# Bias, compression and state space parameters laid out by the host as their tiles lie

## The chip, the cores and the metric

The kernel runs on one core of a Trainium2 chip. The metric is the device time of one execution in microseconds (us), as the median of several runs. A core has five engines that run beside one another: TensorE (PE, matrix products; its weight loads are shown apart as PEld), VectorE (DVE), ScalarE (ACT), GpSimd (POOL) and SyncE (SP), which here issues all transfers between the DRAM and the core's memory. Each engine works through its own instructions in order. What the host does to the inputs before the launch is not in the time.

## The reference

One sequence of 256 positions and 1024 channels passes through seven sublayers, each with a modulated RMS norm ahead of it:

0. mixer AB: a sparse attention (with a compressed branch, a selected and a window branch, weighted by gates) and a sliding-window attention with sink logits; both add a relative bias, `rel_table[bucket(distance)]` by head, with 32 buckets
1. feed-forward (FFN), `(silu(h Wg) * (h Wu)) Wd` with 2816 hidden channels
2. mixer CD: a block attention with relative bias and a stick-breaking attention
3. FFN, and 4. FFN
5. mixer S5: a short convolution and a diagonal complex state space model
6. FFN, then a last norm

The compressed branch of mixer AB joins windows of 32 positions with weights: `kc[n,e] = sum over l,d of (k[16n+l, d] + pe[l, d]) * wk[l, d, e]`, and the same for values. The state space model has 32 groups of 64 states and 16 channels:

```
dt = exp(log_dt);  lam_bar = exp(lam*dt);  b_bar = (lam_bar-1)/lam * b
bu = einsum('gpc,sgc->sgp', b_bar, u);  states = scan(x_t = lam_bar*x_(t-1) + bu_t)
y  = real(einsum('gcp,sgp->sgc', c, states)) + d*u
```

## The kernel before

**Precision and weights.** Most products run in three passes of rounded halves: an operand is split into `whi` (ACT, line 238) and `wlo` (DVE, line 239), and PE makes hi*hi, lo*hi and hi*lo (lines 160 to 162 for column tiles, 498 to 500 for output projections, 812 to 814 and 528 to 531 for `tok` products). Weights come by SP (line 255) into a ring of six buffers `raw` of 8 KB in each partition; four pairs of `whi`/`wlo` are in rotation, so a split runs two or three steps ahead of PE.

**Order.** PE's order is written out by hand: it is the program's order. The other engines' orders are made at build time by a scheduler that simulates the program and issues what is ready first; `issue_after` and `keep_in_program_order` hold single instructions back. A queue `bgq` feeds pieces of the next modulation vectors (`macc`, line 301, from 4 MB of weights for each) between steps, by planned costs.

**Side jobs.** The state space parameters are prepared in a list `extra` of 22 functions that `s5_stages` returns, in this order: `fetch`, `b_fetch` twice, `turn`, `c_fetch`, `steps`, `base`, `factor`, `b_turn` twice, `c_turn` four times, and eight times `table`. In the third FFN (s = 3) the list begins, and `ex(3)` takes the next entry at every third call; it is called once for each of 20 column tiles and 22 output rows of an FFN, so 14 entries are taken in the third FFN and the rest in the fourth. Buffers `big0` to `big2` have one copy each and pass from job to job.

- `fetch` (1190): 10 small transfers, with rows in partitions; `turn` (1204): two PE transpositions bring them into columns, `vec` and `lam`
- `steps` (1221) and `factor` (1244): about 30 operations on 128x16 elements; two exponentials go by a power on POOL (1161)
- `b_fetch` (1265), `b_turn` (1275): B into a zeroed `big0`, eight transpositions, ACT copies, a write to the DRAM copy `bmat`
- `c_fetch` (1286), `c_turn` (1293): C into `big1`, eight transpositions and 24 DVE products with the factor, a write to `cmat`
- `table` (1314): for two state tiles sines and cosines of 256 angles; nine instructions on ACT, five on DVE, a write of 512 KB to `tabs`; its first DVE instruction keeps the program's place (1324)

Mixer S5 reads `bmat`, `cmat` (1346, 1347) and `tabs` back.

**Start and mixer AB.** `start` computes the first norm from streamed modulation weights; inside it `bias_rows` (823) makes the bias by head and distance (16 x 384) with a one-hot product and adds a mask; `bias_store` (830) writes it 33 times to the DRAM copy `rd`, so that `bias_load` (835) can read each row shifted by one, as four transfers of 32 partitions for a tile `T` of four heads. Mixer AB loads four `T`, mixer CD two. After the query and key tiles of the window attention, `setup` (1669) loads `pe`, transposes it on PE, repeats it with a product by `iddup`, and copies it to `pe_parts`; the `tok` products (values and gates) follow, and then the scores (640). `cmp_probs` (1009) copies strided columns of `T` to `tcb` (1013, 1014) on DVE. `compress` (958) loads its two weights as four transfers into two `raw` buffers.

Of the kernel before, what the change touches and what calls it, by code (L numbers as in the profile page):

```python
# [7 lines left out]
F32 = mybir.dt.float32  # L8
# [8 lines left out]
NEG = -1e30  # L17
# [22 lines left out]
def shape_constants(np):  # L40
    c = np.zeros((128, C_W), np.float32)
    p = np.arange(128)
    c[p, C_ID + p] = 1.0
    c[p, C_SW + (p + 64) % 128] = 1.0
    c[:, C_MASK:C_MASK + 128] = np.where(p[None, :] < p[:, None], 0.0, NEG)
    c[:, C_VALID] = p >= 31
    for h in range(8):
        c[:, C_HROW + h] = p // 16 == h
    c[:, C_T:C_T + 16] = np.arange(16)
    c[:, C_T + 16:C_T + 32] = 16 * np.arange(16)  # L50
    d = 255 - np.arange(384)
    n = np.maximum(d, 1)
    big = 16 + (np.log(n / 16.0) / math.log(8.0) * 16).astype(np.int64)
    bucket = np.where(d < 16, np.maximum(d, 0), np.minimum(big, 31))
    oh = np.zeros((32, 384), np.float32)
    ok = d >= 0
    oh[bucket[ok], np.arange(384)[ok]] = 1.0
    m = np.zeros((16, 384), np.float32)
    m[:, d < 0] = NEG
    m[8:, d >= 128] = NEG  # L60
    return c, oh, m


def packed(np, I):
# [36 lines left out]
    for i, (g, u, d) in enumerate([(w[:, :DFF], w[:, DFF:], I["ffn_w_out"][l]) for l, w in enumerate(I["ffn_w_in"])] +  # L101
                                  [tuple(I[f"ffn{n}_w_{x}_2"][0] for x in ("gate", "up", "down")) for n in (1, 2)]):
        for nm, w in (("g", g), ("u", u)):
# [8 lines left out]
                                    for v in range(2)]) for q in range(2)])  # L112
    o["mod_bias"] = np.concatenate([I["mod_b"].reshape(12, D), I["b_mod_2"].reshape(9, D)])
# [3 lines left out]
class Net:  # L117
# [705 lines left out]
    def bias_rows(self, oh, ma, rt):  # L823

        ps = self.bank([384])
        self.nc.tensor.matmul(ps[:16, :], rt, oh, start=True, stop=True)
        self.nc.vector.tensor_tensor(ma, ps[:16, :], ma, ALU.add)
        self.bias = ma

    def bias_store(self):  # L830

        self.rd = self.dp.tile([16, 33, 384], F32, name="rd")
        self.nc.sync.dma_start(out=self.rd, in_=self.bias.unsqueeze(1).to_broadcast([16, 33, 384]))
# [337 lines left out]
    def s5_stages(self, ap, tp):  # L1171
# [18 lines left out]
        def fetch():  # L1190
            vecs = [I["glu_b_2"][0], I["ssm_d_2"][0], I["out_norm_conv_2"][0], I["out_norm_ssm_2"][0]]
            vecs += [I["conv_w_2"][0, k] for k in range(3)]
            for n, v in enumerate(vecs):
                nc.sync.dma_start(out=vr[4 * n:4 * n + 4, :], in_=v.rearrange("(f p) -> f p", p=128))
            for n, k in enumerate(("lambda_re_2", "lambda_im_2")):
                nc.sync.dma_start(out=lr[16 * n:16 * n + 16, :], in_=I[k][0].rearrange("(i g) p -> i (g p)", g=2))
            nc.sync.dma_start(out=ld[32:48, :], in_=I["log_dt_2"][0].rearrange("(i g) -> i g", g=2))
            V.tensor_copy(lr[32:48, :].rearrange("i (g p) -> i g p", g=2),
                          ld[32:48, :].unsqueeze(2).to_broadcast([16, 2, 64]))
# [3 lines left out]

        def turn():
            ps = self.bank([28])
            nc.tensor.transpose(ps, vr, self.c32[:28, C_ID:C_ID + 28])
            V.tensor_copy(vec.rearrange("p a b -> p (a b)"), ps)
            ps = self.bank([3, 16])
            nc.tensor.transpose(ps.rearrange("p a b -> p (a b)"), lr, self.c32[:48, C_ID:C_ID + 48])
            V.tensor_copy(lam, ps)  # L1210
# [54 lines left out]
        def b_fetch(x):  # L1265
            if x == 0:
                bd["b"] = big(0)
                nc.gpsimd.memset(bd["b"], 0.0)
            t = bd[x] = bd["b"][:, 512 * x:512 * x + 512].rearrange("p (i c) -> p i c", i=16)
            k = ("ssm_b_re_2", "ssm_b_im_2")[x]  # L1270
            for g in range(2):
                nc.sync.dma_start(out=t[64 * g:64 * g + 64, :, 16 * g:16 * g + 16],
                                    in_=I[k][0].rearrange("(i g) p c -> g p i c", g=2)[g])

        def b_turn(x):

            ps = self.bank([4, 128])
            for j in range(4):
                nc.tensor.transpose(ps[:, j, :], bd[x][:, 4 * j:4 * j + 4, :].rearrange("p a b -> p (a b)"), self.ident)
            if x == 0:  # L1280
                bd["bm"] = big(2)
            self.evac(bd["bm"][:, 512 * x:512 * x + 512].rearrange("p (a b) -> p a b", a=4), None, ps)
            if x == 1:
                nc.sync.dma_start(out=self.s_b, in_=bd["bm"])

        def c_fetch():
            t = bd["c"] = big(1).rearrange("p (j x d q) -> p j x d q", j=4, x=2, d=2)
            for x, k in enumerate(("ssm_c_re_2", "ssm_c_im_2")):
                for d in range(2):
                    nc.sync.dma_start(out=t[:, :, x, d, :],  # L1290
                                        in_=I[k][0].rearrange("g c p -> (g c) p").rearrange("(j r) p -> r j p", j=4))

        def c_turn(j):

            ps = self.bank([2, 4, 32])
            for x in range(2):
                nc.tensor.transpose(ps[:, x].rearrange("p a b -> p (a b)"),
                                    bd["c"][:, j, x].rearrange("p a b -> p (a b)"), self.ident)
            fb = [f[:, x, 4 * j:4 * j + 4].unsqueeze(2).to_broadcast([128, 4, 32]) for x in range(2)]
            u, v = (part(x).rearrange("p (a b) -> p a b", a=4) for x in range(2))  # L1300
            if j == 0:
                bd["ct"] = big(2)
            c = bd["ct"].rearrange("p (j x a b) -> p j x a b", j=4, x=2, a=4)
            cr, ci = (c[:, j, x] for x in range(2))
            TT(cr, ps[:, 0], fb[0], ALU.mult)
            TT(u, ps[:, 1], fb[1], ALU.mult)
# [488 lines left out]
```

## Time and profile before

| | us |
|---|---|
| median of 3 runs | 1233.86 |
| lowest and highest | 1230.62, 1235.3 |
| the profiled execution | 1234.67 |
| its span, first to last instruction | 1232.2 |
| PE, DVE, ACT, POOL busy | 1176.0, 921.3, 611.0, 136.6 |
| mean granted clock of PE | 0.981 |

All numbers of the trace come from that one execution. Busy times overlap; a busy PE need not be at its full rate. Where a row names a line, it is the line of the instruction in the kernel, often that of a helper.

### The profile page before, as it was taken

Reading aid. Unit: us, or ns where it says so; the run is one execution under the profiler, and the core shown is the slowest. Engines: PE = TensorE matmul, PEld = TensorE weight load, DVE = VectorE, ACT = ScalarE, POOL = GpSimd, SP = SyncE. Lnnn points to the kernel's source line nnn. Section 1 sums busy time; section 2 is a strip of 40 time slices with the busy share of each in tenths; the row PEclk is TensorE's granted clock in tenths of the full one; section 3 lists DMA queues with packets and bytes.
Section 4 is the critical chain, followed back from the end, with each engine's and each line's share of the span. In section 5 each row is a group of like instructions: output and inputs, shape, how many; then the busy total and the mean of one; then the engine's idle time right before and its main releaser. Section 6 shows DMA issues by size and latency. Waiting matters only on the chain.

```text
span 1232.2 us, 19361 instructions
## 1 busy us (share of the span) xinstructions
PE 1176.0 (95%) x7475; PEld 1020.5 (83%) x7475; DVE 921.3 (75%) x1377; ACT 611.0 (50%) x1109; POOL 136.6 (11%) x182
## 2 busy tenths in 40 slices
PE   6889999999999999899999899999999889999997
PEld 2778659999887974799998799998888657999985
DVE  5777848868858787787976799889469967766545
ACT  2356645454454565444444556766443334444433
POOL 2000010000001011102000100000028851000000
PEclk8889999999999999899999999999999889999999
DMA  9996376878865768877787478788654444655520
GB/s 340 299 349 244 145 295 254 301 257 312 327 249 154 297 233 319 271 286 296 286 306 279 154 284 304 274 351 318 243 200 162 166 159 171 239 212 202 203 103 34
DMA packets 62857, 304.33 MB, mean 247 GB/s; under 512 B 16663, under 2 KB 20499, under 8 KB 30382
## 3 DMA queue, kind: packets, MB, share of 16 engines
q1 hardware_dynamic: 62766, 303.11, 67.4%
q8 instruction: 58, 0.95, 0.3%
q14 instruction: 33, 0.27, 0.1%
HBM read 295.97 MB, written 7.11 MB: 246 GB/s over the span
## 4 chain that ended last, share of the span: by engine, by line
PE 62%; issue 17%; DVE 8%; DMA 6%; POOL 4%; ACT 2%; POOLq 0%; SPq 0%; DVEq 0%; ACTq 0%
PE ps L162 11%; PE ps L160 11%; PE ps L161 11%; PE y L500 5%; PE y L498 5%; PE y L499 5%; PE y L496 4%; PE tok L528 2%; DMA raw<-in_ab_cmp_dram 1%; PE ps L640 1%; PE o L684 1%; DVE wlo L239 1%; PE ps L1353 1%; DMA T<-rd 1%; DVE st L1405 1%
## 5 line engine op out<-in xcount | busy, mean ns | idle before, releaser
L238 ACT ACTIVATE whi<-raw 128x1024 fp32r<-128x1024 f32 (+2 forms) x307 | 318.5, 1045 | 376.4 <-PE ps L161 145.0
L239 DVE TENSOR_TENSOR wlo<-raw,whi 128x1024 fp32r<-128x1024 f32 (+2 forms) x307 | 370.2, 1212 | 162.0 <-ACT whi L238 160.7
L162 PE MATMUL ps<-hhi,wlo 128*128 128x256 f32 x1488 | 422.0, 284 | 2.8 <-DVE wlo L239 2.8
L160 PE MATMUL ps<-hhi,whi 128*128 128x256 f32 x1488 | 424.3, 285 | 0.0
L161 PE MATMUL ps<-hlo,whi 128*128 128x256 f32 x1488 | 421.5, 283 | 0.0
L162 PEld LDWEIGHTS ps<-hhi,wlo 128*128 128x128 f32 x1488 | 285.9, 192 | 3.8 <-DVE wlo L239 3.8
L160 PEld LDWEIGHTS ps<-hhi,whi 128*128 128x128 f32 x1488 | 286.1, 192 | 2.9 <-issue 1.7
L161 PEld LDWEIGHTS ps<-hlo,whi 128*128 128x128 f32 x1488 | 286.0, 192 | 1.4 <-DVE wlo L239 0.5
L301 DVE SCALAR_TENSOR_TENSOR macc<-raw,c,macc 128x1024 f32<-128x1024 f32 x152 | 195.1, 1283 | 7.3 <-DMA raw<-in_mod_dram 3.5
L498 PE MATMUL y<-whi,gh 128*128 128x512 f32 x352 | 139.7, 397 | 0.0
L499 PE MATMUL y<-wlo,gh 128*128 128x512 f32 x352 | 138.9, 395 | 0.0
L500 PE MATMUL y<-whi,gl 128*128 128x512 f32 x352 | 138.9, 395 | 0.0
L500 PEld LDWEIGHTS y<-whi,gl 128*128 128x128 f32 x352 | 66.1, 188 | 15.8
L499 PEld LDWEIGHTS y<-wlo,gh 128*128 128x128 f32 x352 | 66.2, 188 | 15.3
L498 PEld LDWEIGHTS y<-whi,gh 128*128 128x128 f32 x352 | 66.2, 188 | 15.3
L291 POOL MEMSET macc<- 128x1024 f32 x19 | 18.7, 984 | 523.7 <-DVE mlo L316 507.8
L496 PE MATMUL y<-raw,o 128*128 128x512 f32 x128 | 57.4, 596 | 1.4 <-ACT o L167 1.4
L381 POOL TENSOR_SCALAR ms<-ss 128x1 f32<-128x1 f32 x24 | 12.3, 512 | 372.9 <-ACT junk L391 368.9
L599 DVE TENSOR_TENSOR g<-sg,ps 128x256 f32<-128x256 f32 x80 | 33.5, 418 | 25.6 <-PE ps L162 25.2
L158 PE MATMUL ps<-h,raw 128*128 128x256 f32 x192 | 45.9, 396 | 5.0 <-DVE cvt L1483 5.0
L158 PEld LDWEIGHTS ps<-h,raw 128*128 128x128 f32 x192 | 37.5, 198 | 11.2 <-DVE cvt L1483 5.2
L496 PEld LDWEIGHTS y<-raw,o 128*128 128x128 f32 x128 | 23.4, 190 | 28.0 <-issue 25.6
(335 smaller groups left out, 1492.5 us busy)
## 6 DMA issues: line engine op xcount, KB each, us to landing
raw<-in_mod_dram SPq DMA_DIRECT2D x76, 1024.0 KB
raw<-in_ffn_g_dram SPq DMA_DIRECT2D x44, 1024.0 KB
raw<-in_ffn_u_dram SPq DMA_DIRECT2D x44, 1024.0 KB
raw<-in_ffn_d_dram SPq DMA_DIRECT2D x44, 1024.0 KB
raw<-in_ab_out_dram SPq DMA_DIRECT2D x8, 1024.0 KB
raw<-in_cd_out_dram SPq DMA_DIRECT2D x8, 1024.0 KB
raw<-in_s_c_dram SPq DMA_DIRECT2D x6, 1024.0 KB
raw<-in_s_out_dram SPq DMA_DIRECT2D x6, 1024.0 KB
```

The costliest lines, as they stand in the source:

```text
L158: mm(out, lh, rh, start=first, stop=last)
L160: mm(out, lh, rh, start=first, stop=False)
L161: mm(out, lh, rl, start=False, stop=False)
L162: mm(out, ll, rh, start=False, stop=last)
L238: self.nc.scalar.activation(hv, src, AF.Copy)
L239: self.nc.vector.tensor_tensor(lv, src, hv.bitcast(F32), ALU.subtract)
L301: nc.vector.scalar_tensor_tensor(acc, box["r"][:, kk % 2], c[:, kk:kk + 1], acc, ALU.mult, ALU.add)
L496: mm(ys[h][b], xh[:, k, c], wh[:, 0, sl], start=first, stop=last)
L498: mm(ys[h][b], xh[:, k, c], wh[:, 0, sl], start=first, stop=False)
L499: mm(ys[h][b], xh[:, k, c], wl[:, 0, sl], start=False, stop=False)
L500: mm(ys[h][b], xl[:, k, c], wh[:, 0, sl], start=False, stop=last)
L599: nc.vector.tensor_tensor(g, sg, pu, ALU.mult)
```

## The change

The host lays out seven more arrays: the whole bias tiles (`bias`, 4 x 128 x 4 x 256, masks included), `cmp_pe`, `cmp_w`, the vectors `s5_vec`, `s5_lam`, and B and C of the state space model in the form in which the tiles lie. The kernel loads them as they are. `bias_rows`, `bias_store`, the chain for `pe`, `turn`, `b_fetch` and `b_turn` go; `c_turn`'s four entries become one `c_times` on whole tiles, without transposition. The list of side jobs has 14 entries: `fetch`, `c_fetch`, `steps`, `base`, `factor`, `c_times`, eight times `table`.

```
@@ packed: host side
+    d = np.arange(128)[:, None] - np.arange(256)[None, :] + 128
+    n = np.maximum(d, 1)
+    big = 16 + (np.log(n / 16.0) / math.log(8.0) * 16).astype(np.int64)
+    bucket = np.where(d < 16, np.maximum(d, 0), np.minimum(big, 31))
+    t = I["rel_table"][bucket].transpose(0, 2, 1).astype(np.float32)
+    t = np.where((d < 0)[:, None], np.float32(NEG), t)
+    t[:, 8:] = np.where((d >= 128)[:, None], np.float32(NEG), t[:, 8:])
+    o["bias"] = t.reshape(128, 4, 4, 256).transpose(1, 0, 2, 3)
+
+    o["cmp_pe"] = I["nsa_cmp_pe"][0].reshape(2, 8, 2, 64).transpose(2, 3, 1, 0).reshape(128, 8, 2)
+    o["cmp_w"] = np.stack([I[k][0].reshape(2, 8, 2, 64, 64).transpose(2, 3, 1, 0, 4).reshape(128, 1024)
+                           for k in ("nsa_cmp_wk", "nsa_cmp_wv")], 1)[None]
+
+    vecs = [I["glu_b_2"][0], I["ssm_d_2"][0], I["out_norm_conv_2"][0], I["out_norm_ssm_2"][0], *I["conv_w_2"][0]]
+    o["s5_vec"] = np.stack([v.reshape(4, 128) for v in vecs]).transpose(2, 0, 1)
+    pair = lambda a: a.reshape(16, 128).T
+    o["s5_lam"] = np.stack([pair(I["lambda_re_2"][0]), pair(I["lambda_im_2"][0]),
+                            pair(np.repeat(I["log_dt_2"][0], 64))], 1)
+    b = np.zeros((4, 2, 16, 2, 4, 2, 64), np.float32)
+    ct = np.zeros((2, 64, 16, 2, 2, 16), np.float32)
+    for x, k in enumerate(("ssm_b_re_2", "ssm_b_im_2")):
+        v = I[k][0].reshape(4, 4, 2, 64, 16)
+        for g in range(2):
+            b[:, g, :, x, :, g] = v[:, :, g].transpose(1, 3, 0, 2)
+    for x, k in enumerate(("ssm_c_re_2", "ssm_c_im_2")):
+        ct[:, :, :, x] = I[k][0].reshape(16, 2, 16, 64).transpose(3, 0, 1, 2)[None]
+    o["s5_b"], o["s5_cm"] = b.reshape(128, 1024), ct.reshape(128, 1024)
@@ bias
-    def bias_rows(self, oh, ma, rt):
...
-    def bias_store(self):
...
     def bias_load(self, h0, bufs):
...
-        a = self.rd[h0:h0 + 4]
-        for i in range(4):
-            src = bass.AP(tensor=a.tensor, offset=a.offset + 127 - 32 * i, ap=[[383, 32], [33 * 384, 4], [1, 256]])
-            self.nc.sync.dma_start(out=T[32 * i:32 * i + 32], in_=src)
+        self.nc.sync.dma_start(out=T, in_=self.I["bias"][h0 // 4])
         return T
@@ compress
-        for ca, w in ((kp, I["nsa_cmp_wk"][0]), (vp, I["nsa_cmp_wv"][0])):
-            r = self.raw()
-            for h2 in range(2):
-                nc.sync.dma_start(
-                    out=r[:, :1024].rearrange("p (k h e) -> p k h e", k=8, h=2)[:, :, h2, :],
-                    in_=w[16 * h2:16 * h2 + 16].rearrange("(k l) d e -> (l d) k e", l=2))
+        w = self.load(I["cmp_w"][0])
+        for ca, r in ((kp, w[:, 0]), (vp, w[:, 1])):
@@ s5_stages
...
+            nc.sync.dma_start(out=vec, in_=I["s5_vec"])
+            nc.sync.dma_start(out=lam, in_=I["s5_lam"])
...
-        def turn():
...
-        def b_fetch(x):
...
-        def b_turn(x):
...
         def c_fetch():
...
-        def c_turn(j):
...
+            bd["c"] = big(1)
+            nc.sync.dma_start(out=bd["c"], in_=I["s5_cm"])
+        def c_times():
+            c0 = bd["c"].rearrange("p (i x b) -> p i x b", i=16, x=2)
+            ct = big(2)
+            c1 = ct.rearrange("p (j x a b) -> p j x a b", j=4, x=2, a=4)
+            u, v = (t.rearrange("p (i b) -> p i b", i=16) for t in (lambda b: (b[:, :512], b[:, 512:]))(big(0)))
+            fb = [f[:, x, :].unsqueeze(2).to_broadcast([128, 16, 32]) for x in range(2)]
+            four = lambda t: t.rearrange("p (j a) b -> p j a b", j=4)
+            TT(u, c0[:, :, 0], fb[0], ALU.mult)
+            TT(v, c0[:, :, 1], fb[1], ALU.mult)
+            TT(c1[:, :, 0], four(u), four(v), ALU.subtract)
+            TT(u, c0[:, :, 0], fb[1], ALU.mult)
+            TT(v, c0[:, :, 1], fb[0], ALU.mult)
+            V.scalar_tensor_tensor(c1[:, :, 1], four(u), -1.0, four(v), ALU.mult, ALU.subtract)
+            nc.sync.dma_start(out=self.s_c, in_=ct)
...
-        res = [fetch, lambda: b_fetch(0), lambda: b_fetch(1), turn, c_fetch, steps, base, factor,
-               lambda: b_turn(0), lambda: b_turn(1)]
-        res += [lambda j=j: c_turn(j) for j in range(4)]
+        res = [fetch, c_fetch, steps, base, factor, c_times]
@@ mixer_s5
-            nc.sync.dma_start(out=bm.rearrange("p x j q -> p (x j q)"), in_=self.s_b)
+            nc.sync.dma_start(out=bm.rearrange("p x j q -> p (x j q)"), in_=I["s5_b"])
@@ start
-            oh, ma = (self.np_.tile([128, 512], F32, tag="ht", name=n, bufs=3) for n in ("oh", "ma"))
-            bias = oh[:32, :384], ma[:16, :384], oh[:32, 384:400]
-            for t, n in zip(bias, ("onehot", "bandmask", "rel_table")):
-                nc.sync.dma_start(out=t, in_=I[n])
...
-            self.bias_rows(*bias)
...
-            self.bias_store()
@@ setup
...
+        self.pe_parts = ap.tile([128, 8, 2], F32, name="pf")
+        nc.sync.dma_start(out=self.pe_parts, in_=I["cmp_pe"])
```

## Rows read from the trace of the kernel before

**Rows 1.** The page: busy time by engine, the chain's shares, one costly group (count, busy us, mean ns).
```profile
PE 1176.0 (95%) x7475; PEld 1020.5 (83%) x7475; DVE 921.3 (75%) x1377; ACT 611.0 (50%) x1109; POOL 136.6 (11%) x182
...
PE 62%; issue 17%; DVE 8%; DMA 6%; POOL 4%; ACT 2%; POOLq 0%; SPq 0%; DVEq 0%; ACTq 0%
...
L238 ACT ACTIVATE whi<-raw 128x1024 fp32r<-128x1024 f32 (+2 forms) x307 | 318.5, 1045 | 376.4 <-PE ps L161 145.0
```

**Rows 2.** The chain of waits, 0 to 260 us: start us, us, what.
```profile
33.21 18.25 DMA raw<-in_ab_cmp_dram
51.47 9.69 DMA T<-rd
```

**Rows 3.** Stage table: window, busy of PE, PEld, DVE, ACT, POOL; granted clock, DMA share, GB/s.
```profile
40.00:45.00 5.00, 4.00 (x31) 3.65 (x32) 3.65 (x7) 1.83 (x3) 0.91 (x4) 1.00 0.95 196
55.00:60.00 5.00, 4.38 (x14) 4.11 (x15) 2.76 (x7) 0.00 (x0) 0.00 (x0) 0.53 0.88 177
60.00:65.00 5.00, 5.00 (x23) 4.93 (x22) 2.05 (x3) 2.12 (x2) 0.00 (x0) 0.79 1.09 256
70.00:75.00 5.00, 5.00 (x44) 5.00 (x43) 4.80 (x17) 3.40 (x7) 0.00 (x0) 1.00 1.01 419
```

**Rows 4.** PE in order of time, 50 to 69 us: start, us, line, [idle before <-releaser].
```profile
55.00 0.19 PE L1679 MATMUL ps<-c,pe 32*64 32x32 f32 x1 [2.45 <-DMA pe<-in_nsa_cmp_pe_dram]
...
56.37 0.71 PE L812 MATMUL tok<-whi,hhi 128*128 128x408 f32 x1
...
62.41 0.35 PE L812 MATMUL tok<-whi,hhi 128*128 128x408 f32 x1
...
67.82 0.34 PE L814 MATMUL tok<-whi,hlo 128*128 128x408 f32 x1
68.09 1.16 PE L640 MATMUL ps<-kb,qb 64*128 64x128 f32 x16
```

**Rows 5.** DVE in order of time, 0 to 130 us.
```profile
59.44 1.28 DVE L301 SCALAR_TENSOR_TENSOR macc<-raw,c,macc 128x1024 f32<-128x1024 f32 x1 [2.22 <-DMA raw<-in_mod_dram]
...
65.98 0.22 DVE L1013 COPY tcb<-T 128x60 f32<-128x60 f32 x1 [3.93 <-DMA T<-rd]
...
86.49 1.25 DVE L669 TENSOR_SCALAR p<-p,st 128x128 f32<-128x128 f32 x6
```

**Rows 6.** POOL in order of time, 480 to 530 us.
```profile
497.90 0.95 POOL L1268 MEMSET big<- 128x1024 f32 x1 [9.68 <-PE y L496]
498.80 0.95 POOL L291 MEMSET macc<- 128x1024 f32 x1
499.84 0.30 POOL L381 TENSOR_SCALAR ms<-ss 128x1 f32<-128x1 f32 x1
```

**Rows 7.** PE in order of time, 484 to 526 us.
```profile
506.39 1.94 PE L414 MATMUL ps<-c,ht 128*128 128x128 f32 x8 [2.81 <-DVE ht L406]
```

**Rows 8.** Stage table, 505 to 515 us.
```profile
505.00:510.00 5.00, 3.61 (x16) 3.41 (x17) 4.89 (x8) 1.20 (x2) 0.00 (x0) 0.58 0.92 239
510.00:515.00 5.00, 5.00 (x34) 5.00 (x33) 3.10 (x4) 0.25 (x1) 0.00 (x0) 0.73 0.96 177
```

**Rows 9.** PE in order of time, 643 to 648 us.
```profile
645.48 0.40 PE L499 MATMUL y<-wlo,gh 128*128 128x512 f32 x1
645.72 0.40 PE L500 MATMUL y<-whi,gl 128*128 128x512 f32 x1
645.96 0.60 PE L1279 MATMUL ps<-c,big 128*128 128x128 f32 x4
646.31 0.48 PE L498 MATMUL y<-whi,gh 128*128 128x512 f32 x1
```

**Rows 10.** Stage table, 720 to 870 us, instructions on big alone.
```profile
720.00:870.00 150.00, 0.00 (x0) 0.00 (x0) 20.15 (x40) 37.45 (x68) 0.00 (x0) 1.00 0.84 317
```

**Rows 11.** Stage table, 640 to 690 us.
```profile
640.00:690.00 50.00, 50.00 (x225) 40.29 (x224) 31.91 (x44) 22.18 (x26) 0.95 (x1) 1.00 0.73 268
```

**Rows 12.** POOL in order of time, 565 to 720 us.
```profile
575.77 2.91 POOL L1161 TENSOR_TENSOR dt<-ebase,lam 128x16 f32<-128x16 f32 x1 [71.51 <-DVE lam L1210]
```

More of the change, by code (lines that the diff above doesn't have):

```diff
@@ L50, in shape_constants @@
     c[:, C_T + 16:C_T + 32] = 16 * np.arange(16)
[L51 to L61, printed above, removed]
+    return c
 def packed(np, I):
@@ L821, in tok_items @@
         return [(lambda k0=k0: prepare(k0), lambda ws, k0=k0: run(k0, ws)) for k0 in range(0, 8, nk2)]
-    def bias_rows(self, oh, ma, rt):
[L825 to L828, printed above, removed]
-    def bias_store(self):
-        self.rd = self.dp.tile([16, 33, 384], F32, name="rd")
-        self.nc.sync.dma_start(out=self.rd, in_=self.bias.unsqueeze(1).to_broadcast([16, 33, 384]))
     def bias_load(self, h0, bufs):
         T = self.ap.tile([128, 4, 256], F32, tag="T", name="T", bufs=bufs)
-        a = self.rd[h0:h0 + 4]
-        for i in range(4):
-            src = bass.AP(tensor=a.tensor, offset=a.offset + 127 - 32 * i, ap=[[383, 32], [33 * 384, 4], [1, 256]])
-            self.nc.sync.dma_start(out=T[32 * i:32 * i + 32], in_=src)
+        self.nc.sync.dma_start(out=T, in_=self.I["bias"][h0 // 4])
         return T
@@ L1177, in s5_stages @@
         big = lambda x: tp.tile([128, 1024], F32, tag=f"big{x}", name=f"big{x}")
-        vr, lr, ld = part(0)[:28], part(1)[:48], tp.tile([48, 2], F32, name="ld")
         vec = self.s_vec = ap.tile([128, 7, 4], F32, name="vec")
         r = self.s_r = ap.tile([128, 16], F32, name="r")
-        self.s_b, self.s_c = (self.dp.tile([128, 1024], F32, name=n) for n in ("bmat", "cmat"))
+        self.s_c = self.dp.tile([128, 1024], F32, name="cmat")
         self.tabs = self.dp.tile([16, 128, 512], F32, name="tabs")
@@ L1190, in fetch @@
         def fetch():
[L1191 to L1199, printed above, removed]
+            nc.sync.dma_start(out=vec, in_=I["s5_vec"])
+            nc.sync.dma_start(out=lam, in_=I["s5_lam"])
             V.memset(hpi, math.pi / 2)
@@ L1202, in fetch @@
             V.memset(magic[:, 1:2], -MAGIC)
-        def turn():
[L1205 to L1210, printed above, removed]
         def trig(psi, s, c, t):
@@ L1263, in factor @@
                 TT(f[:, x], f[:, x], m, ALU.mult)
-        def b_fetch(x):
[L1266 to L1273, printed above, removed]
@@ L1275, in b_turn @@
-        def b_turn(x):
[L1277 to L1284, printed above, removed]
-        def c_fetch():
[L1287 to L1291, printed above, removed]
@@ L1293, in c_turn @@
-        def c_turn(j):
[L1295 to L1306, printed above, removed]
-            TT(cr, cr, u, ALU.subtract)
-            TT(ci, ps[:, 0], fb[1], ALU.mult)
-            TT(v, ps[:, 1], fb[0], ALU.mult)
-            V.scalar_tensor_tensor(ci, ci, -1.0, v, ALU.mult, ALU.subtract)
-            if j == 3:
-                nc.sync.dma_start(out=self.s_c, in_=bd["ct"])
+        def c_fetch():
+            bd["c"] = big(1)
+            nc.sync.dma_start(out=bd["c"], in_=I["s5_cm"])
@@ L1674, in setup @@
         nc.vector.tensor_tensor(self.iddup, self.c32[:, C_ID:C_ID + 128], self.c32[:, C_SW:C_SW + 128], ALU.add)
-        pe = ap.tile([32, 64], F32, name="pe")
-        nc.sync.dma_start(out=pe, in_=I["nsa_cmp_pe"][0])
-        ps = self.bank([32])
-        nc.tensor.transpose(ps[:64, :], pe, self.c32[:32, C_ID:C_ID + 32])
-        pt = ap.tile([64, 32], F32, name="pet")
-        nc.vector.tensor_copy(pt, ps[:64, :])
-        ps = self.bank([32])
-        nc.tensor.matmul(ps, self.iddup[:64, :], pt, start=True, stop=True)
-        pf = ap.tile([128, 8, 2], F32, name="pf")
-        for l2 in range(2):
-            sl = slice(64 * l2, 64 * l2 + 64)
-            nc.vector.tensor_copy(pf[sl], ps[sl].rearrange("p (h k l) -> p k h l", h=2, k=8)[:, :, :, l2])
-        self.pe_parts = pf
+        self.pe_parts = ap.tile([128, 8, 2], F32, name="pf")
+        nc.sync.dma_start(out=self.pe_parts, in_=I["cmp_pe"])
     def run(self, upto=99):
@@ L1757, in net_kernel @@
         Net(ctx, tc, I, out, dbg).run(upto)
[L1760 to L1763 removed]
+_INS = ['x', 'c', 'norm_w', 'swa_sinks', 'cond_2', 'ffn1_norm_2', 'mix_norm_2', 'ffn2_norm_2', 'final_norm_2']
 def build(inputs, dbg=None, upto=99):
@@ L1780, in build @@
         add(name, np.ascontiguousarray(a))
-    for name, a in zip(("consts", "onehot", "bandmask"), shape_constants(np)):
-        add(name, a)
+    add("consts", shape_constants(np))
     out = nc.dram_tensor("out_0_dram", (1, S, D), F32, kind="ExternalOutput").ap()
```

4 lines of the change are left out of this document (removed).

## The prediction

> **What bounds the kernel now.** I read the page first, then the chain of waits, then stage tables, then the order of time on single engines. The page shows TensorE (PE) busy for 1176 of 1232.2 us, and the chain of waits puts 62% of the span on PE and 6% on DMA [rows 1]. So most of the span is matmuls that this change does not touch, and a saving counts only where PE stands still or issues something that goes. There are three such places.
>
> The first is the start. From 33 to 66 us the chain runs through two transfers: the first weights of the compression branch, then the bias tiles `T` read back from the DRAM copy `rd` [rows 2]. In the stage table the DMA engines are full there but move little: 177 and 256 GB/s while `T` comes in, 196 GB/s while `rd` is written, against 419 GB/s at 70 to 75 us, when only weights come [rows 3]. On PE the reader sees a wait of 2.45 us for `pe`, two small products, and then 48 `tok` products, the first of them at the lower clock level: 0.53 was granted from 55 to 60 us, after PE's pause [rows 3, 4]. On VectorE (DVE) the reader sees a copy out of `T` that waited 3.93 us; DVE issues in order, so a split of weights stands behind it [rows 5].
>
> The second is the border between the second mixer and the third feed-forward (FFN), at 498 to 515 us, where PE waits 2.81 us for `ht` [rows 7] and then is granted 0.58 and 0.73 of its clock, means over its two levels of 1.2 and 2.4 GHz [rows 8]. The third is the third FFN, where PE never stands and each transposition costs its own time [rows 9].
>
> **The change, part by part.** *Start.* The product and the add that make the bias row, its 33-fold write to DRAM (792 KB), 12 of the 16 reads of `T` in this stage (four of 128 KB become one of 512 KB), the transposition and the product for `pe`, and their copies go. One load of 8 KB takes the place of the `pe` chain; it feeds only `ca` on DVE, much later. What does PE gain? Its wait began at 55.00 - 2.45 = 52.55 us and the first `tok` product started at 56.37: 3.82 us go. The 48 `tok` products then took 68.09 - 56.37 = 11.72 us. At full clock they are (67.82 - 62.41)/29 = 0.187 us apart, so 48 take 8.96 us, and 2.76 us go if no pause lowers the clock. PE would reach the first score products 6.6 us earlier [rows 4]. DVE has to keep up, and it has 3.93 us of waiting for `T` and 2.22 us of waiting for modulation weights to give, both behind the slow transfers: 6.15 us [rows 5]. Do the transfers give that? From 40 to 45 us 0.98 MB moved; without the 0.81 MB of `rd` the rest takes 0.4 us at 419 GB/s, a gain of 4.6. From 55 to 65 us 2.17 MB moved, which takes 5.2 us at that rate, a gain of 4.8 [rows 3]. `T` would land some 9.4 us earlier, at about 56.6 us, ahead of its use. I take the smaller of the two engines' gains, **6.2 us**. Bounds: 2.5 us, the `pe` wait alone, if DVE's order puts the copies of `T` or `ca` still further forward and waits there; 9.4 us, all of the transfer time.
>
> The Trainium skill, "DMA: Bandwidth & Descriptors", section "Specifications", says that 512 bytes or more per transfer are enough for full rate. The pieces of `T` are 1 KB (256 values of 4 bytes), so by that rule the wider rows gain nothing and only `rd` does: `T` lands at about 61.4 us, DVE still waits about 1.5 us, and the sum below comes 1.5 us less, to 1228. The trace here speaks against the rule, with 177 and 256 GB/s at a full DMA share [rows 3], though other small transfers are in the same windows.
>
> The compression weights (1 MB) come as one load in one buffer of the ring of six, where two half-filled ones were used. Nothing waited for them, so 0. In the second mixer eight reads of `T` become two. The bytes are the same and the chain there runs through PE and DVE, so 0; at most the 3.93 us that this tile cost in the first mixer [rows 5].
>
> *Border at 500 us.* Eighteen small transfers of state space parameters become three, and the POOL memset of `big` (0.95 us) goes. It and a second memset ran ahead of `ms`, whose input was ready before them: 499.84 would be 498.9 [rows 6]. That is 0.9 us of the chain to `ht`, and a copy of 0.1 us on DVE goes as well: **1.0 us**. Above, if the shorter wait spares the clock, up to 5 x 0.42 + 5 x 0.27 = 3.5 us more [rows 8]. Below: the first exponential on POOL took 2.91 us and could not start before a PE transposition gave it `lam`, after 71.51 us of idle POOL [rows 12]. Now `lam` comes by a transfer and nothing holds this step back. It can fall right here, before the second `ms`, and cost up to 2.9 us. I leave both out of the sum and in the range.
>
> *Transpositions in the third FFN.* 18 go: 2 for the vectors, 8 for B, 8 for C. Four of them put 646.31 - 645.72 = 0.59 us between two products that otherwise start 0.24 us apart: 0.35 us, 0.09 us each [rows 9]. 18 x 0.09 = **1.6 us**. PE is the bound there, so all of it counts; bounds 0.7 (the two groups of four alone) and 2.5 (seven groups, each at the price of four). B needs no work on the core any more and its write to DRAM goes; six DVE operations on 512 columns replace 24 on 128, on a DVE that has 18 of 50 us free [rows 11]. 0.
>
> *The eight tables move.* The list of side jobs falls from 22 entries to 14, and one is taken at every third step of the FFN loops, 14 in each FFN. Tables 1 to 8 were entries 15 to 22 and all lay in the fourth FFN, most of them in its first part, whose steps are longer. They become entries 7 to 14, all in the third FFN, seven of them in its output part, where a step is 12 products of 0.233 us and three steps take 8.4 us. ScalarE (ACT) spent 37.45 us on 68 of the 72 instructions of eight tables, so 4.96 us each; DVE 20.15/8 = 2.5 us [rows 10]. From 640 to 690 us ACT was busy for 22.18 us and has 27.8 us free. Six tables, one in 8.4 us, need 29.8 us [rows 11]. ACT is then full, and about one table slips into the border behind, where PE waits for ACT and DVE. I charge **1.5 us**; bounds 0 (it fits the gaps) and 7.5 us (one table's 4.96 + 2.5 in series). The fourth FFN gets lighter, but PE was never idle in its loops: 0.
>
> **Sum.** 6.2 + 1.0 + 1.6 - 1.5 = 7.3 us. The profiled execution took 1234.67 us for a span of 1232.2; less 7.3 it is 1227.4. It lies 0.8 us above the median of the runs, so against the median I predict 1226.5 us.
>
> **Rivals.** *A, the start is bound by DVE anyway.* Between 70 and 75 us DVE is busy for 4.80 of 5 us, and its run of work ends only with the copies at 86.49 us [rows 3, 5]. If these are tied to DVE's whole load and not to when `T` came, only 2.5 us are gained and the sum is 3.6: 1230. For it: the high share. Against: the 6.15 us of waits just ahead. Chance 0.22.
>
> *B, the clock is spared too.* The wait at 506 us gets shorter than 2.81 us and the clock stays up, worth up to 3.5 us. 7.3 + 3.5 = 10.8 us: 1223. For it: the low clock follows right behind that wait [rows 7, 8]. Against: the exponential on POOL may lengthen the wait. Chance 0.18.
>
> *C, slower: the tables hold up the splits.* ACT issues in order. Where its order has a table's step ahead of a split, and that step waits for its partner on DVE, ACT loses the 2.5 us as well. Three steps then ask for 4.96 + 2.5 + 3 x 1.05 of splits [rows 1] + 0.5 of other work (22.18 less 18 splits, for 8.4 of 50 us) = 11.1 us, against 8.4 that PE takes. Six times 2.7 is 16 us; two steps of buffered weights hide some 5.6; a last table in series adds 5; the gains of 8.8 come off: +7, 1241. It decides as soon as a table needs more than about 4.7 us of ACT's order per 8.4 us. For it: ACT is full already by my own count. Against: a step whose partner is not ready is usually placed later. Chance 0.10.
>
> The forecast keeps 0.50. What a measurement of this kernel can tell from no change is about 0.5%, 6.2 us here, so the line lies at 1227.7. Of the forecast's 0.50 some 0.34 lie below it, of B all, of A 0.03: faster 0.55. Slower is 0.08 out of C and 0.01 elsewhere; the same keeps 0.36. The range runs from B with the start, the transpositions and the tables at their better bounds (3.2, 0.9 and 1.5 us more), 1217, to halfway between A and C, 1236. The likeliest case's own is 1222 to 1231.
>
> **What would show it.** Right: the first score products start near 61.5 us and not 68.09; no wait for `T` on DVE; `tok` products 0.187 us apart from the first on; no write of 792 KB; POOL's first `ms` of the border within 0.3 us of its input; no transpositions between the FFN's products; the side jobs' eight tables all written before the border at 693 us or just behind it, and that border about 1.5 us longer. Wrong: the first score products earlier, but the end of the first mixer not; an exponential on POOL ahead of `ms`; PE waiting for `wlo` in the output part of the third FFN. A time above 1231 would mean that the start's gain was given back, above 1236 that the tables decide.

## The result and the profile after

The changed kernel takes 1218.11 us (median of 4 runs, 1217.92 to 1219.78) against 1233.18 for the kernel before beside it: ratio 0.9882, 95% interval 0.986 to 0.9903. A second comparison (below) gave 0.990 (0.9881 to 0.9919), so the gain is 12 to 15 us. Forecast were 7.3. The profiled execution took 1217.92 us for a span of 1216.1. Runs of one kernel lie up to 10 us apart, and a profile shows only one of them. I therefore take sizes from medians and ratios and use profiles to see where time goes.

The page after, busy time and chain (columns as in [rows 1]):

```profile
PE 1160.1 (95%) x7452; PEld 1010.3 (83%) x7452; DVE 919.3 (76%) x1352; ACT 609.2 (50%) x1107; POOL 136.1 (11%) x181
...
PE 63%; issue 18%; DVE 10%; POOL 3%; ACT 3%; DMA 3%; SPq 0%; POOLq 0%; DVEq 0%; ACTq 0%
```

DMA fell from 6% to 3% of the chain. PE after, in order of time, answers to [rows 4] and [rows 7]:

```profile
51.06 0.35 PE L830 MATMUL tok<-whi,hhi 128*128 128x408 f32 x1
...
60.10 0.72 PE L658 MATMUL ps<-kb,qb 64*128 64x128 f32 x8
...
75.39 0.66 PE L694 MATMUL ps<-c,p 128*128 128x128 f32 x4 [1.56 <-ACT p L685]
...
107.42 0.44 PE L1026 MATMUL ps<-c,sT 128*128 128x128 f32 x2 [2.14 <-ACT sT L1019]
...
167.44 1.04 PE L432 MATMUL ps<-c,ht 128*128 128x128 f32 x8
...
490.79 0.41 PE L432 MATMUL ps<-c,ht 128*128 128x128 f32 x2 [0.72 <-DVE ht L424]
...
499.52 0.38 PE L180 MATMUL ps<-hhi,wlo 128*128 128x256 f32 x1 [0.94 <-DVE wlo L257]
...
682.71 0.69 PE L432 MATMUL ps<-c,ht 128*128 128x128 f32 x2 [4.54 <-DVE ht L424]
...
883.78 0.33 PE L432 MATMUL ps<-c,ht 128*128 128x128 f32 x1
```

The rows of before at the same steps that were not shown yet:

```profile
85.26 0.33 PE L676 MATMUL ps<-c,p 128*128 128x128 f32 x1 [3.44 <-ACT p L667]
86.82 0.47 PE L676 MATMUL ps<-c,p 128*128 128x128 f32 x1 [1.22 <-DVE p L669]
...
180.93 1.04 PE L414 MATMUL ps<-c,ht 128*128 128x128 f32 x8
...
517.13 0.39 PE L162 MATMUL ps<-hhi,wlo 128*128 128x256 f32 x1 [0.52 <-DVE wlo L239]
...
700.17 1.07 PE L414 MATMUL ps<-c,ht 128*128 128x128 f32 x6 [1.53 <-DVE ht L406]
...
899.17 0.33 PE L414 MATMUL ps<-c,ht 128*128 128x128 f32 x1
```

Differences of these starts, before less after, make the ledger. To the score products 68.09 - 60.10 = 8.0 us; to the first `ht` behind the first mixer 13.5; to the third FFN's first split 517.13 - 499.52 = 17.6; to where PE stops behind that FFN (start less wait) 698.64 - 678.17 = 20.5; behind the fourth FFN 15.4; at the end 16.1. So the start gave 13.5, the border at 500 us 4.1, the third FFN 2.9, and 5.1 were lost behind it.

The stage table of before, then of after (columns as in [rows 3]), shows the clock behind the score products:

```profile
85.00:90.00 5.00, 3.51 (x16) 2.60 (x18) 4.06 (x13) 1.10 (x3) 0.00 (x0) 0.60 0.99 395
90.00:95.00 5.00, 5.00 (x33) 4.26 (x30) 3.16 (x21) 1.96 (x8) 0.00 (x0) 0.72 0.82 264
105.00:110.00 5.00, 5.00 (x25) 3.80 (x25) 4.83 (x11) 1.79 (x3) 0.00 (x0) 0.66 0.85 326
```

```profile
85.00:90.00 5.00, 5.00 (x45) 4.91 (x43) 3.86 (x11) 4.17 (x13) 0.95 (x1) 1.00 0.02 7
90.00:95.00 5.00, 5.00 (x38) 4.18 (x38) 3.79 (x5) 1.68 (x3) 0.00 (x0) 1.00 0.11 17
105.00:110.00 5.00, 2.86 (x13) 1.42 (x11) 3.95 (x23) 3.51 (x15) 0.00 (x0) 1.00 0.99 359
```

DVE copies out of `T` without a wait (3.93 us in [rows 5]), and POOL at the border has `ms` 0.1 us behind the memset, the exponential behind the second `rstd` and not ahead of it ([rows 6]):

```profile
53.69 0.21 DVE L1012 COPY tcb<-T 128x60 f32<-128x60 f32 x1
```

```profile
484.39 0.95 POOL L309 MEMSET macc<- 128x1024 f32 x1 [9.67 <-PE y L514]
485.44 0.30 POOL L399 TENSOR_SCALAR ms<-ss 128x1 f32<-128x1 f32 x1
...
489.30 0.56 POOL L401 TENSOR_TENSOR rstd<-ms,neghalf 128x1 f32<-128x1 f32 x1
489.83 2.91 POOL L1160 TENSOR_TENSOR dt<-ebase,lam 128x16 f32<-128x16 f32 x1
```

DVE at the same border, before and then after, with the second pair of `ht` and a product `g`, which have changed places:

```profile
504.79 0.42 DVE L599 TENSOR_TENSOR g<-sg,tok 128x256 f32<-128x256 f32 x1 [1.35 <-ACT sg L598]
...
505.49 1.41 DVE L406 SCALAR_TENSOR_TENSOR ht<-ht,rstd,mod 128x512 f32<-128x512 f32 x2
```

```profile
489.89 1.42 DVE L424 SCALAR_TENSOR_TENSOR ht<-ht,rstd,mod 128x512 f32<-128x512 f32 x2 [0.69 <-POOL rstd L401]
...
492.51 0.41 DVE L617 TENSOR_TENSOR g<-sg,tok 128x256 f32<-128x256 f32 x1
```

### The profile page after: what moved, and what is told of

Read it like the earlier page. It is cut to its first block, busy times and chain, and to the rows that moved or that the text cites. A ratio compares the mean times of both kernels' runs of the same rounds, so it can differ in the third digit from the quotient of the medians.

```text
span 1216.1 us, 19237 instructions
## 1 busy us (share of the span) xinstructions
PE 1160.1 (95%) x7452; PEld 1010.3 (83%) x7452; DVE 919.3 (76%) x1352; ACT 609.2 (50%) x1107; POOL 136.1 (11%) x181
## 4 chain that ended last, share of the span: by engine, by line
PE 63%; issue 18%; DVE 10%; POOL 3%; ACT 3%; DMA 3%; SPq 0%; POOLq 0%; DVEq 0%; ACTq 0%
PE ps L180 11%; PE ps L178 11%; PE ps L179 11%; PE y L518 5%; PE y L516 5%; PE y L517 5%; PE y L514 4%; PE tok L546 2%; DVE macc L319 2%; DVE wlo L257 1%; PE ps L1305 1%; PE ps L658 1%; DVE st L1357 1%; PE o L702 1%; PE ps L432 1%
## 5 line engine op out<-in xcount | busy, mean ns | idle before, releaser
L518 PEld LDWEIGHTS y<-whi,gl 128*128 128x128 f32 x352 | 66.6, 189 | 15.4
```

Of the source, the lines that this page charges most:

```text
L518: mm(ys[h][b], xl[:, k, c], wh[:, 0, sl], start=False, stop=last)
```

## The experiments

Ratios are to the kernel before on the same chip, with 95% intervals; `ht` is the start of the first `ht` product behind the first mixer, and the clock is the mean from 40 to 180 us, both of the one profiled run.

| kernel | median us | ratio | ht | clock |
|---|---|---|---|---|
| before | 1231 to 1233 | 1 | 180.93 | 0.94 |
| whole change, second comparison | 1218.52 | 0.990 (0.9881, 0.9919) | 167.08 | 0.99 |
| start only | 1221.33 | 0.9908 (0.9883, 0.9933) | 168.19 | 0.99 |
| state space only | 1234.15 | 1.0021 (1.0005, 1.0037) | 179.48 | 0.95 |
| pe only | 1230.97 | 0.9993 (0.9976, 1.0009) | 174.32 | 0.98 |
| bias only | 1226.18 | 0.995 (0.9929, 0.9972) | 171.97 | 0.98 |
| bias and pe | 1219.86 | 0.991 (0.9891, 0.993) | 169.03 | 0.99 |
| whole, T from an image | 1219.24 | 0.990 (0.988, 0.992) | 169.10 | 0.96 |
| whole, write kept | 1223.54 | 0.9925 (0.9907, 0.9944) | 171.36 | 0.98 |
| all but bias | 1223.91 | 0.9933 (0.9915, 0.9951) | 174.25 | 0.98 |
| all but pe | 1222.02 | 0.9919 (0.9898, 0.9939) | 173.93 | 0.96 |
| all but bias, held | 1226.88 | 0.9962 (0.9946, 0.9977) | 174.33 | 0.96 |
| write kept, held | 1224.74 | 0.9948 (0.9929, 0.9968) | 171.11 | 0.98 |
| pe only, held | 1230.35 | 0.9997 (0.9981, 1.0014) | 173.80 | 0.98 |
| whole, held | 1226.34 | 0.9962 (0.9944, 0.998) | 177.01 | 0.93 |
| whole, held, filled | 1223.39 | 0.9927 (0.9913, 0.994) | 169.47 | 0.99 |
| before, filled | 1230.92 | 0.9998 (0.9985, 1.0012) | 176.21 | 0.99 |
| whole, tables late | 1215.86 | 0.9873 (0.9851, 0.9895) | 170.12 | 0.99 |
| whole, tables split | 1216.72 | 0.9869 (0.9848, 0.989) | 167.67 | 0.99 |

### Which part carries the gain

**Start only, state space only.** The two halves of the change's own diff, each on the kernel before.

```diff
 start only:        + bias, cmp_w, cmp_pe;   s5_stages, mixer_s5 as before
 state space only:  + s5_vec, s5_lam, s5_b, s5_cm;   the rest as before
```

> The edits of the start alone (bias, compression weights, pe from the host); the state space stages as before. Theory M (the start's gain is 13.5 us, read at the first ht product behind the first mixer, 180.93 before and 167.44 after; half of it are waits for transfers, half the clock that no longer falls and softmax waits that shrink with them): that product at 167.5, no low clock ahead of it, and the border at 506 as before (wait 2.81 us, low clock behind it). Time 1233.2 - 13.5 = 1219.7. Rival F (the forecast's 6.2 us, and the rest of the whole change's gain comes out of the state space part): the product near 175, time 1227.

> The state space edits alone; the start as before. Theory M: border wait 2.81 to 0.7 and no low clock behind it (-4.0), transpositions -2.4, border to the fourth FFN +4.4 by the eighth table: sum -2.0, time 1231. Rival F (the terms of the forecast: -1.0, -1.6, +1.5): 1232. Rival N (the low clock behind the border is tied to where the start left the pattern, and not to this wait): low clock stays at about 506, time 1233. The border wait and the low clock tell M and N apart.

The start alone gives 11 us with `ht` at 168.19, as theory M had it, and it keeps the wait of 3.16 us at the border. The state space part does at the border what M said (a wait of 0.71 us, a clock of 1.00), but as a whole it is 0.2% slower and not 2 us faster: behind the third FFN it has the whole change's wait of 4.54 us for `ht`, with all tables in that FFN. The halves sum to some 9 us, with intervals of 3 and 2 us either way; the whole has 12 to 15. The rest is not explained.

**The whole again.**

> The whole change once more, on the chip of the runs beside it, for comparison: 1218 within 2 us. If the whole is worth no more than its two halves measured alone (-11.2 and +1.7 us), it is 1223.

1218.52: the first measurement holds. In this second profile of the same kernel the clock from 90 to 95 us is 0.71, where the first has 1.00, and `ht` comes no later for it.

**pe only, bias only, both.**

```diff
 pe only, bias and pe:
-        pe = ap.tile([32, 64], F32, name="pe")
...
+        nc.sync.dma_start(out=self.pe_parts, in_=I["cmp_pe"])
 bias only, bias and pe:
-            self.bias_store()
...
+        self.nc.sync.dma_start(out=T, in_=self.I["bias"][h0 // 4])
```

> Before, with only pe's transposed copy from the host: no PE wait for pe at 55 us, no two products; rd and T go through DRAM as before. Theory M (T and the streams behind it set what follows): tok starts 3.8 us earlier, at 52.6, but T lands as late as before, so the softmax waits behind the score products grow by about as much; at the first ht product behind the first mixer at most 2 us remain, time 1231 to 1233. Rival P (the PE pause for pe is what brings the low clock and all that follows): ht product at 170 or earlier, time 1222.

> Before, with only the bias from the host: no rd, T by one load; pe still goes through its transposition and product. Theory M: the transfers were what held pe back too, so the wait for pe falls under 0.7 us; two products and a copy stay (about 1.4 us); no low clock in the mixer; first ht product at about 169, time 1221. Rival P (the pe wait matters by itself): pe wait stays near 2.4 us, low clock at 55, ht product near 176, time 1228.

> Before, with bias and pe from the host; compression weights by four transfers and state space stages as before. Theory M (the forecast's 0 for the compression weights): like the start alone, 1221. Rival Q (the two edits alone gave -1.5 and -6.3, the rest of the -11.2 comes from the compression weights): 1224.5, and a wait in the mixer behind 100 us that the start alone does not have.

pe alone gains nothing that can be measured, bias alone 6 us, both 11. The compression weights are worth 0, as forecast: both without them do as well as the start with them. With bias only, PE no longer waits for the load of `pe`, yet it waits as long one step later, for a copy on DVE that stands behind splits. M's 0.7 us was wrong:

```profile
53.85 0.63 PE L1691 MATMUL ps<-pet,iddup 64*128 64x32 f32 x2 [2.48 <-DVE pet L1688]
```

**All but pe, all but bias.** The same parts taken out of the whole.

```diff
 all but pe:    setup as before
 all but bias:  bias_rows, bias_store, bias_load as before
```

> The whole change without pe: its transposition, product and copies as before. pe now lands early, but its first copy stands on VectorE behind splits of weights and a modulation sum: PE waits about 2.5 us ahead of the second product, the clock falls, the score products start 5 us later than in the whole change (65 and not 60 us); first ht product at 171, time 1223. Rival (the pause is given back by later waits, as 2 us are at sT): 168.5, 1219.5.

> The whole change without the bias: product, write and reads of T as before; pe, compression weights and state space parameters from the host. Theory H: VectorE waits for T again (over 2 us behind 58 us), first ht product at 174 to 176, time 1225. Rival (the pe wait is the larger part once the rest is gone): ht product at 170, 1221.

Without pe the same 2.48 us of waiting stand there; the whole loses 2 to 3.5 us (by ratios 0.9919 and 0.990, by medians). Without bias it loses 4 to 5. But PE reaches the score products at 61.25, only 1.2 us behind the whole, although `T` lands late (DVE waits 2.08 us for it). So where do the 4 to 5 us go?

### Write, reads and the order on DVE

**T from an image; write kept.**

```diff
 image:
-        self.nc.sync.dma_start(out=T, in_=self.I["bias"][h0 // 4])
+        a = self.I["bias"][h0:h0 + 4]      # the host's 16 x 33 x 384
+        for i in range(4):
+            src = bass.AP(tensor=a.tensor, offset=a.offset + 127 - 32 * i, ap=[[383, 32], [33 * 384, 4], [1, 256]])
+            self.nc.sync.dma_start(out=T[32 * i:32 * i + 32], in_=src)
 write kept:  bias_rows and bias_store as before, T by one load
```

> The whole change, but the host gives the image of 16 x 33 x 384 that was written to DRAM before, and each T is read from it by four transfers with a step of 383, in pieces of 1 KB; nothing is written. It tells the write from the reads. Theory W (the write, and the wait for it, is what held the streams): T lands at most 2 us later than with one load, 1219. Rival N (the reads in pieces of 1 KB are slow, as 177 and 256 GB/s in the trace of before had it): the streams behind T come 5 us later, first ht product behind the first mixer at 172 and not 167.4, time 1223.

> The whole change, but the bias row's product, add and the 33-fold write to DRAM stay as before; T comes by one load from the host, and what is written is read by nobody. Theory H (write and reads in pieces each take some 4.7 us from the weight streams, and the streams have about that much to spare in the mixer; only both together are late): product and add cost 1 us, first ht product behind the first mixer at 168.5 to 170, time 1219.5. Theory W (the write alone is what held the streams): first ht product at 173, time 1223.

The stage table of the image kernel, then of the whole, while `T` comes in:

```profile
45.00:50.00 5.00, 5.00 (x44) 5.00 (x43) 4.10 (x4) 3.65 (x7) 0.00 (x0) 1.00 1.04 195
50.00:55.00 5.00, 5.00 (x32) 4.99 (x31) 3.73 (x7) 2.22 (x3) 0.00 (x0) 1.00 0.99 248
```

```profile
45.00:50.00 5.00, 5.00 (x44) 5.00 (x44) 4.07 (x4) 3.74 (x7) 0.00 (x0) 1.00 1.04 406
50.00:55.00 5.00, 5.00 (x33) 4.99 (x32) 4.37 (x9) 2.22 (x3) 0.00 (x0) 1.00 1.03 427
```

With these reads DMA does move about half as much: 1.95 MB less in these 10 us, 4.7 us at 415 GB/s, which is the forecast's 4.8. They cost no time that can be measured (1219.24 against 1218.52 us). The likely reason is that DMA runs below its full share later in the mixer (0.37 and 0.13 from 85 to 95 us in the image kernel), so that the streams can catch up; no run tests that.

That the pieces of 1 KB are what halves the rate is not shown. Each of these transfers also fills only 32 partitions, where the one load fills 128, and no run changes one without the other. The packets in the trace of the image kernel speak against the length alone. Its 2048 packets of 1 KB in the first mixer took 78 ns in the median but 44 ns at the least, which on 16 engines would be 372 GB/s, an estimate. And packets of 8 KB that started beside them, from 52 to 54 us, were slow as well: 527 ns in the median, against 309 over the whole run. The Trainium skill ("DMA: Bandwidth & Descriptors", "Specifications") has full rate from 512 bytes on. The prediction took the low rates as speaking against that rule; by these packets they do not refute it.

Keeping the write cost 3 to 5 us, and the number is theory W's, but the place is not. PE starts the scores at 61.02 and loses its time at 116 us. PE and DVE of the kernel with the write kept:

```profile
116.53 0.66 PE L1065 MATMUL ps<-c,pc 128*128 128x128 f32 x2 [3.68 <-DVE pc L1058]
```

```profile
107.68 0.48 DVE L1049 TENSOR_TENSOR pc<-ps,tcb 128x128 f32<-128x128 f32 x2
108.08 1.28 DVE L329 SCALAR_TENSOR_TENSOR macc<-raw,c,macc 128x1024 f32<-128x1024 f32 x1
...
110.25 1.28 DVE L329 SCALAR_TENSOR_TENSOR macc<-raw,c,macc 128x1024 f32<-128x1024 f32 x1
```

Two modulation sums stand inside the softmax of the compressed branch. The build-time scheduler put them there. The same wait of 3.68 us is in pe only and in all but bias, the other two that have the write, no pe chain and no hold on the sums, and in no other profile.

**Sums held.** In four kernels the sums are ordered behind that softmax, with the whole change as control.

```diff
-                    with self.behind(kk == 0):
+                    with self.behind(kk == 0), self.held():   # issue_after the last step of pc
```

> The whole change without the bias, with the modulation sums of the first mixer held behind the compressed branch's softmax. Theory O (the loss was the order on VectorE): no wait of 3.68 us near 117 us, first ht product behind the first mixer at 169.5 and not 174.3, time 1219.5. Rival T (T's late landing is the loss and shows up at a later wait): ht product still at 173 or later, 1223.

> The whole change with product, add and write of the bias kept and read by nobody, sums held as above. Theory O: no wait of 3.68 us, first ht product at 168.5, time 1219.5. Rival T: 1223 as without the hold.

> Before with pe alone from the host, sums held. Theory O: the 3.68 us wait and the low clock behind it go, so pe alone is worth about 6 us: 1226. Rival T: 1231 as without the hold.

> The whole change with the sums held: control. No sum stood inside that softmax, so 1218.5 as the whole change, within 1 us; if the hold itself gains (waits for sT of 2.14 us and for zr of 0.6 us go, which four sums ahead of them cause), up to 2.5 us less, 1216; if it pushes the sums to a later wait, more.

Theory O's times failed: the 3.68 us went in all three, and nothing got faster. But the hold has a price of its own, since the control lost some 8 us. Against this control (0.9962) the kept write (0.9948) and the missing bias (0.9962) cost nothing, where without the hold they cost 3 to 5 us. So the cost of the write depends on the order on DVE. Whether that order is all of it stays open, because all four held kernels share two new waits. PE of the control, held:

```profile
116.91 0.33 PE L699 MATMUL ps<-c,p 128*128 128x128 f32 x1 [1.31 <-ACT p L690]
117.72 0.69 PE L699 MATMUL ps<-c,p 128*128 128x128 f32 x2 [0.48 <-DVE p L692]
```

### Waits and the clock

**Filled.** Products that nobody reads, put into the waits: 10 and 3 into the two above; in the kernel before, 20 and 5 at `pe`, 28 and 10 at the first two transpositions of `p`.

```diff
         for r in range(4):
+            if r < len(more):
+                self.filler(ps[:, 2:4], more[r])     # ones_r by hh, 256 columns
             self.nc.tensor.transpose(ps[:, r, :], ...)
```

> The whole change with the sums held, and 10 + 3 products into an unused half of the bank right ahead of the transposition that waits 1.31 us and the one that waits 0.48 us (near 117 us). They take about the time of the wait, so nothing is gained by PE itself. Theory K (the pause brings the low clock, and that is the loss): no low clock from 117 to 135, first ht product behind the first mixer at 168 and not 177, time 1219. Rival L (the loss is DVE's later order; the clock only shows it): ht product at 175 or later, 1225.

> The kernel before, with products that nobody reads in four waits of the first mixer: 20 and 5 at pe, 28 and 10 at the first two transpositions of p. The waits for data stay. Theory K: no low clock from 50 to 110 (20 us in the profile of before: 2.8, 2.2 and 2.1 us lost), first ht product at 174 and not 181, time 1231.2 - 7 = 1224. Rival L: the waits for T and the late streams hold PE anyway and what the clock gives back goes into longer waits: 1230.

Stage table of the held kernel, then of the filled one:

```profile
115.00:120.00 5.00, 3.21 (x14) 2.25 (x13) 4.21 (x12) 3.49 (x11) 0.00 (x0) 0.76 0.80 274
120.00:125.00 5.00, 5.00 (x11) 2.72 (x10) 2.53 (x13) 2.76 (x10) 0.00 (x0) 0.50 0.33 136
125.00:130.00 5.00, 5.00 (x14) 3.46 (x13) 2.50 (x8) 2.15 (x6) 0.95 (x1) 0.50 0.00 1
130.00:135.00 5.00, 5.00 (x19) 3.80 (x18) 3.15 (x8) 2.28 (x6) 0.00 (x0) 0.54 0.21 28
```

```profile
115.00:120.00 5.00, 4.74 (x31) 3.96 (x31) 4.67 (x14) 3.74 (x13) 0.00 (x0) 1.00 0.78 256
120.00:125.00 5.00, 5.00 (x21) 3.19 (x20) 4.13 (x14) 3.50 (x11) 1.07 (x1) 1.00 0.40 167
125.00:130.00 5.00, 5.00 (x28) 3.77 (x27) 4.33 (x14) 3.86 (x11) 0.02 (x1) 1.00 0.01 2
```

Behind two waits of 1.8 us together PE was at its lower level (0.50, 1.2 GHz) from 120 to 130 us; with filled waits the clock stays at 1.00 and `ht` starts 7.5 us earlier, as theory K had it. The time lies between the theories' 1219 and 1225: the medians differ by 3 us only, 1226.34 and 1223.39, and the ratios by 4. The runs of the held kernel lie between 1222.1 and 1232.3, and the profiled one, 1228.78, is among the slower ones.

The waits are not the whole of it. The three other held kernels have the same two waits, but their clock is at 0.53 to 0.58 in the lowest 5 us and back at 1.00 by 130 us. And in the image kernel it falls although PE has no wait from 75.4 to 109 us:

```profile
90.00:95.00 5.00, 5.00 (x25) 3.86 (x25) 3.68 (x5) 0.55 (x1) 0.00 (x0) 0.64 0.13 17
95.00:100.00 5.00, 5.00 (x23) 4.45 (x22) 4.88 (x20) 1.83 (x6) 0.00 (x0) 0.50 0.87 357
```

That kernel's `ht` comes only 2 us later than in the whole change, and its time is the same. Part of what the low clock costs goes into a wait that shrinks: PE waits 0.48 us for `sT` there and 2.14 in the whole change.

In the kernel before, the fillers raise the clock (0.94 to 0.99) and `ht` comes 4.7 us earlier in the profile; the median is as before (-0.2 to +0.1%). Of that, 2.4 us went at a wait for `wlo` in the fourth FFN, 2.91 us where 0.52 stood. So for the kernel before, K is shown in the profile and not in the time.

### The tables

**Late; split.**

```diff
-        return res + [lambda i=i: table(i) for i in range(0, 16, 2)]
+        return res + [lambda: None] * 8 + [eight tables]                         # late
+        return res + [four tables] + [lambda: None] * 6 + [four tables]          # split
```

> The whole change, with eight empty entries put ahead of the tables in the list of side jobs, so that the eight tables are taken in the fourth FFN as before the change. Theory M (the eighth table's steps stand among the border's steps on ScalarE and VectorE; the wait for ht of 4.54 us and the low clock behind it are its price): that wait back to 1.5 us, no low clock near 690, 4.4 us faster than the whole change: 1213.7. Rival F (the forecast's price of the move, 1.5 us): 1216.6. Rival G (the tables cost the same in the fourth FFN, where the first weights are waited for): 1218.

> The whole change, with four tables taken in the third FFN, then six empty entries, then four tables in the fourth. In the trace of the whole change a table takes 10.8 us from write to write, so that five are written ahead of the border and three behind it or in it. Theory S (only tables that stand in the border cost): wait for ht at the border 1.5 us, like all tables in the fourth FFN, 1215.5. Rival (each table in the third FFN costs, by splits held up): between that and the whole change, 1217.

Both are faster than the whole change, by 3 to 4 us in the ratios (0.9873 and 0.9869 against 0.990) and 2 to 3 in the medians. The intervals overlap a little; the slowest run of either, 1218.17 and 1218.36, is near the fastest of the whole change, 1217.92. In both profiles the wait of 4.54 us for `ht` is 1.42. The split kernel speaks for tables costing nothing inside the third FFN; those that stand in the border cost. They are the best versions, and equal within the measurement. SP's issues of the tables' writes in the whole change:

```profile
663.93 0.38 SPq L1282 DMA_DIRECT2D tabs<-big  x1
674.16 0.38 SPq L1282 DMA_DIRECT2D tabs<-big  x1
685.12 0.37 SPq L1282 DMA_DIRECT2D tabs<-big  x1
695.18 0.38 SPq L1282 DMA_DIRECT2D tabs<-big  x1
714.42 0.38 SPq L1282 DMA_DIRECT2D tabs<-big  x1
```

One comes every 10 to 11 us until 695 us, and three, the last of these rows, lie behind the FFN's end at 678 us. The stage table of the whole change there, with the clock:

```profile
675.00:680.00 5.00, 3.17 (x14) 2.25 (x12) 4.64 (x9) 5.00 (x13) 1.40 (x3) 1.00 0.28 106
680.00:685.00 5.00, 2.29 (x10) 2.20 (x11) 4.84 (x8) 4.39 (x8) 1.79 (x2) 0.55 0.00 0
685.00:690.00 5.00, 5.00 (x30) 4.52 (x29) 4.50 (x9) 4.56 (x9) 1.89 (x3) 0.77 0.82 250
```

## Why the prediction was right in direction and too small

The sign and the range were right; the gain is about twice the forecast. That the range held is partly luck: its lower end, 1217, was added up from a start of 9.4 us and tables at no cost, and both came out otherwise. By its steps:

- **Start, 6.2 us: the term that was mis-sized.** It measures 11 us (start only; bias and pe), 13.5 in the pair of profiles. Up to the score products it held: forecast 6.6, measured 8.0 in the pair and 7.2 with the start alone, the `tok` products at full clock from the first on. The step that failed is the next one, "I take the smaller of the two engines' gains, 6.2 us": it closed the account at the score products. Behind them PE waited 3.44 and 1.22 us for `p`, now 1.56, and ran at 0.60, 0.72 and 0.66 of its clock, now at 1.00. The prediction has this stretch only in rival A, as work of DVE that would stay. Of the 13.5 us, 5.5 come from there, after 1.7 given back at the wait for `sT` (0.47 us before, 2.14 after). How they divide between waits and clock is open: filled waits bring 4.7 us in a profile of before, no difference in its median.
- **Its reason, transfers of 9.4 us,** was right in size for the reads (4.7) and wrong in effect: they cost no measurable time. The write, left in the whole change, costs 3 to 5 us, and not through `T`, which lands in time there; the cost goes when the order on DVE is held, but how the order makes it is open. What pe costs, with the bias from the host, is a copy on DVE behind splits, not the wait for its load. The two hide one another: alone 1 and 6 us, together 11.
- **Compression weights 0, second mixer 0:** right (second: 380.71 - 180.93 = 199.8 us from `ht` to `ht` before, 199.7 after).
- **Border at 500 us, 1.0 us:** 4.1 in the profile. 0.9 is POOL's `ms`, as forecast. 1.2 more came on DVE, where a product `g` that had waited 1.35 us for ACT no longer stands ahead of `ht`. The last 2 are the clock, rival B's mechanism, 0.58 and 0.73 before, 1.00 now (2.4 us, of which 0.4 go again at the wait for `wlo`). The other profiles bear this out: in the 13 with a border wait of 0.7 to 0.9 us no low clock follows there, and in the seven with 2.8 to 3.3 us it does in six. The kernel with pe only is the exception, 3.03 us and a clock of 1.00. The feared exponential fell behind the second `ms`.
- **Transpositions, 1.6 us:** 2.9 between the rows of the ledger, beyond the bound of 2.5. If all of it is theirs, one costs 0.16 us and not 0.09.
- **Tables, +1.5 us:** 5.1 in the profile; 2 to 4 by the kernels with late and split tables. "About one table slips" was wrong: three do. ACT was not full (37.73 of 50 us from 622 to 672); one table takes 10 to 11 us, near rival C's 11.1, most likely because its steps on ACT and DVE wait for one another. But PE has no wait for a split from 615 to 676 us: C's rate was right, its place was not.

## What to carry to other kernels

When a stall goes, follow PE to the next point where all engines meet again, with the granted clock of each stage behind it, before closing the sum. A slow transfer is worth what its stream lacks, not what it takes: look for unused DMA share later in the stage. Where a build-time scheduler sets the order, removing one step moves others, so measure parts both alone and left out of the whole.

## What was not expected of the hardware

- Two waits of 1.31 and 0.48 us on PE were followed by a granted clock of 0.50 over 10 us, and `ht` came some 9 us later than in the whole change; with products in the waits the clock stayed at 1.00. In another kernel the clock fell to 0.50 with no wait ahead of it.
- Whether the clock falls at a given place differs between runs of one program: 1.00 and 0.71 from 90 to 95 us in the two profiles of the whole change. The held kernel's 12 runs spread over 10 us, with mean clocks from 0.981 to 0.987.
- While `T` came in by transfers of 32 partitions, in pieces of 1 KB, DMA moved 195 to 248 GB/s at a full share; one transfer of 128 partitions, 4 KB in each, left 406 to 427. Single 1 KB packets took 44 to over 100 ns, so the length alone is not shown to be the reason.
